# The first group of a projection by seven products, and four fills placed apart

## The chip, the cores and the metric

The kernel runs on one NeuronCore of a Trainium2 chip. Five engines work side by side: TensorE (PE) multiplies matrices, VectorE (DVE) and ScalarE (ACT) work element by element, GpSimd (POOL) and SyncE (SP) mostly start transfers (DMAs). Each engine runs its own instructions strictly in the order in which the program lists them, and semaphores make it wait for others. The metric is the device time of one execution in microseconds (us); lower is better.

## The reference, cut to what matters

One layer of a streaming encoder: six column blocks of one large product of the input x (1024 x 1024) with w_in (1024 x 6144), two mixers on four of them, gates from the other two, an output product and a layer norm.

```python
h = jnp.einsum('bsd,de->bse', x, w_in[l]) + b_in[l]
xa, za, xb, zb, ga, gb = jnp.split(h, splits, axis=-1)
xa = _causal_depthwise_conv(xa, conv_w[l], conv_b[l])
ya = _rg_lru(xa, ...) * jax.nn.silu(za)
yb = _multiscale_pool(xb, w_pool[l], b_pool[l], pool_scale[l]) * jax.nn.silu(zb)
merged = (jax.nn.sigmoid(ga) * jnp.einsum('bsw,wd->bsd', ya, w_proj_a[l])
          + jax.nn.sigmoid(gb) * jnp.einsum('bsw,wd->bsd', yb, w_proj_b[l]))
y = jnp.einsum('bsd,de->bse', merged, w_out[l]) + b_out[l]
x = _layer_norm(DEEPNORM_ALPHA * x + y, ln_gain[l], ln_bias[l])
```

All of it is float32. The kernel keeps that precision by splitting every operand into a high and a low part (high x high, high x low, low x high), so that one product of a 128 x 128 weight block with 512 columns of the input is three matmuls.

## The kernel before

**Groups and seven products.** The large product is cut into 24 groups, listed in `order` (line 601): G0, A0, G1, A1, G2 and so on, then the B groups. A group takes two column blocks of 128 of w_in (`blocks_of`, line 606), each 1024 rows long. With the two halves of the rows as k and the two halves of the 1024 input columns as h, a group is a 2 x 2 by 2 x 2 block product, and it is computed in Strassen's way (Winograd's form) with seven products instead of eight. Each of the seven is four quarters of 128 rows by three passes: 12 matmuls. `Group` (line 530) has them as m1 to m7; m1 and m2 use parts of the weights and the input as they are (blocks 11, and 12 with 21), the others use sums. `Weights` (line 475) makes the weight sums: `step("12")` splits the first raw block `ra`, `step("75")` makes two sums with the second block `rb` and splits them, `step("63")` two more, `step("4")` splits a part of `rb`. A split (line 456) is a cast on ACT for the high part and a subtraction on DVE for the low part. The sums of the input are made once, in the opening, and are used by all groups. What PSUM holds is added up in `a_outputs`, `g_outputs` and `b_outputs` (functions c11, c12, c21, c22), on DVE for the most part; `copied` (line 540) copies PSUM to SBUF on ACT.

**The opening (lines 956 to 1136).** Eight matmuls on zeros (`WARM`) run while the first input lands. G0 is not computed with seven products but plainly: four blocks of weight (`w0r`, split into `w0h`, `w0l`) and four parts of the input in quarters as they arrive, 2 x 2 x 8 x 3 = 96 matmuls into four PSUM banks `ps_s` (`mm0`, `parts`), whose outputs ACT reads directly (`plain`, line 833). Meanwhile DVE and ACT split the input (`x13`, `x2`, `xb`) and make its sums (`t13` for products 5 and 7, `t24` for 6 and 4). Then A0 follows: products 1, 2, 5, 7 and 3 in the opening, 6 and 4 between the products of G1 (`first_rest`).

**The loop (line 1157).** For every further group: weights of the next group, products 1, 2, 7, then the work put off from earlier groups (`between`: gate matmuls `ps_g` of an A group, product 3 of the group before, its end), then products 6, 4, 5. `run_jobs` hands two or three jobs per group to POOL: sums of weight and input blocks in DRAM by adding DMAs. Among the jobs is the input plus the output bias, which the last stage needs: a fill of a DRAM tile `xb` of 1 MB with the bias row (on the SP queue), then an adding DMA of x (on POOL), four times; two of the pairs are queued behind the first weight sums, two behind the group of A3 (`biased_input`, lines 702 and 796).

**What sets the order.** `Plan` (line 162) records all operations, gives each a due time and lays them out in a simulated time. TensorE and POOL keep the order of the program. On ACT, DVE and SP the operation that is due first among those that are ready goes next; `within` (line 180) and `LEAD` set how long an operation may be put off. Its costs are formulas in `cost` (line 220), with a rate of 270 GB/s for the SP queue. The result is one fixed list per engine; on the chip an engine never changes it. Buffers are few: 28 tiles of 4 KB per partition in the pool x, 10 in w, 4 in r, 10 in k (1024 columns of work), 4 of half the size in e, and 8 PSUM banks. A tile that is written waits until the earlier user of its buffer is done, and a store to DRAM counts as a use.

Of the kernel before, what the change touches and what calls it, by code (L numbers as in the profile page):

```python
# [26 lines left out]
WARM = 8  # L27
# [134 lines left out]
class Plan:  # L162
# [10 lines left out]
    @contextmanager  # L173
    def in_order(self, *engines):
        self.chained.append(set(engines))
        yield
        self.chained.pop()
# [229 lines left out]
def layer_kernel(ctx: ExitStack, tc: tile.TileContext, xq, x, w_in, par, wg, w_pool, wpa, wpb, w_out, rows, out):  # L407
# [67 lines left out]
    class Weights:  # L475


        def __init__(self, name, w1, w2):
            self.name, self.out, self.tiles = name, {}, {}
            self.ra, self.rb = rt(f"ra_{name}"), rt(f"rb_{name}")  # L480
            nc.sync.dma_start(self.ra, w1)
            nc.sync.dma_start(self.rb, w2)
# [219 lines left out]
    def biased_input(blocks):  # L702
        for sl in HALF if not src.get("bias") else ():
            src["bias"] = True
# [3 lines left out]
            nc.sync.dma_start(bias_d[:, sl], t)  # L708
        for i in blocks:
# [53 lines left out]
    def a_gates(c, xc, xh, xl, sz):  # L763
# [29 lines left out]
        if c == KQ - 1:  # L793
            input_sums1("a")
            output_sums()
            biased_input((0, 1))
        elif c == NK - 1:
            input_sums2("a")

# [3 lines left out]
    def g_outputs(sec, d):  # L803
# [5 lines left out]
        def c11(ps, m1):  # L809
            V.tensor_tensor(t[0][:, HALF[0]], ps, m1, ALU.add)  # L810

        def c12(ps, rest=None):
            if rest is not None:
                V.tensor_tensor(rest, ps, rest, ALU.add)
                ps = rest
# [11 lines left out]
        def finish():  # L827
            done(0, 0, t[0][:, HALF[0]], 1.0)
            store(0)
# [3 lines left out]
        def plain(i, ps):  # L833
            for h in range(2):
                done(i, h, ps[h], 1.0)
            store(i)
# [4 lines left out]
        finish.plain = plain  # L841
# [114 lines left out]
    begin = ctx.enter_context(ExitStack())  # L956
    pass
# [3 lines left out]
    for i in range(WARM):  # L961
        nc.tensor.matmul(psw, warm[:, 0:P], warm, start=True, stop=True)
    first = blocks_of(*order[0])
    wr, wh, wl = [[f(f"{t}{n}") for n in range(2)] for t, f in
                  (("w0r", lambda n: wt(n, F32)), ("w0h", wt), ("w0l", wt))]
# [4 lines left out]
    xb = [xt(f"xb_{q}") for q in range(KQ)]  # L970

    def w0_part(t, n, a, b):
        return t[n].rearrange("p h (k m) -> p h k m", m=P)[:, :, a:b, :]

    def dma_w0(n, a, b):

        (A if a == 0 else nc.sync).dma_start(w0_part(wr, n, a, b), w_in[first[n]].rearrange("p (h k) m -> p h k m", h=2)[:, :, a:b, :])

    def split_w0(n, a, b):
        split(*(w0_part(t, n, a, b) for t in (wr, wh, wl)))  # L980

    def dma_x(q, i, sl=slice(0, S)):
        nc.sync.dma_start(xr[q][i][:, sl], xq[q, i][:, sl])


    def quarter(q, kh, h):
        if kh == h:
            return x13[q][0][:, kh, :], x13[q][1][:, kh, :]
        t = x2[q] if kh else xb[q]
        return t[:, 0, :], t[:, 1, :]  # L990

    raws = {(0, 0): (0, 0), (1, 1): (0, 1), (0, 1): (1, 0), (1, 0): (1, 1)}

    def split_x(q, kh, h):
        i, p = raws[kh, h]
        split(xr[q][i][:, HALF[p]], *quarter(q, kh, h))

    ps0 = [[bank(f"ps_s{n}_{h}") for h in range(2)] for n in range(2)]

    def mm0(q, kh, h, n):  # L1000
        sl = slice(q * P, (q + 1) * P)
        passes(ps0[n][h], (wh[n][:, kh, sl], wl[n][:, kh, sl]), quarter(q, kh, h),
               q == 0 and kh == h, q == KQ - 1 and kh != h)

    dma_w0(0, 0, 1)
    dma_x(0, 0, HALF[0])
    dma_w0(1, 0, 1)
    dma_x(0, 0, HALF[1])
    dma_x(0, 1, HALF[0])
    dma_x(0, 1, HALF[1])  # L1010
    dma_w0(0, 1, KQ)
    dma_x(1, 0)
    dma_w0(1, 1, KQ)
    dma_x(1, 1)
    for q in range(2, KQ):
        dma_x(q, 0)
        dma_x(q, 1)
    nc.sync.dma_start(par_sb, par)
    softplus()

    X = {j: [None] * KQ for j in range(1, 8)}
    t13, t24 = [None] * KQ, [None] * KQ
    for q in range(KQ):
        X[1][q], X[2][q], X[3][q] = quarter(q, 0, 0), quarter(q, 1, 0), quarter(q, 1, 1)

    x57 = [[xt(f"x57{t}{q}") for t in "hl"] for q in range(KQ)]
    x64 = [[xt(f"x64{t}{q}") for t in "hl"] for q in range(KQ)]
    for q in range(KQ):
        for i, (a, b) in enumerate(((5, 6), (7, 4))):
# [3 lines left out]
    def hi(raw, t):  # L1033
        A.copy(t, raw)

    def lo(raw, t, u):
        V.tensor_tensor(u, raw, t.bitcast(F32), ALU.subtract)

    def sum57(q):
        t13[q] = xt(f"t13_{q}", F32)  # L1040
        r = xr[q][0].rearrange("p (i s) -> p i s", i=2)
        V.tensor_tensor(t13[q], r, xr[q][1][:, HALF[0]].unsqueeze(1).to_broadcast((P, 2, H)), ALU.subtract)

    def hi57(q):
        hi(t13[q], x57[q][0])

    def lo57(q):
        lo(t13[q], *x57[q])

    def sum6(q):  # L1050
        t24[q] = wt(f"t24_{q}", F32)
        V.scalar_tensor_tensor(t24[q][:, 0, :], t13[q][:, 0, :], -1.0, xr[q][0][:, HALF[1]], ALU.mult, ALU.subtract)

    def sum4(q):
        V.scalar_tensor_tensor(t24[q][:, 1, :], t24[q][:, 0, :], -1.0, xr[q][1][:, HALF[1]], ALU.mult, ALU.subtract)

    def hi64(q, i):
        hi(t24[q][:, i, :], x64[q][0][:, i, :])

    def lo64(q, i):  # L1060
        lo(t24[q][:, i, :], *(t[:, i, :] for t in x64[q]))

    def parts(q, between=None):
        r = xr[q][0].rearrange("p (i s) -> p i s", i=2)
        todo = [(r, *x13[q])] + [(xr[q][raws[p][0]][:, HALF[raws[p][1]]], *quarter(q, *p)) for p in ((0, 1), (1, 0))]
        if between is not None:
            split(*todo.pop(0))
            between()
        for raw, t, u in todo:
            hi(raw, t)  # L1070
        for raw, t, u in todo:
            lo(raw, t, u)
        for kh, h in ((0, 0), (1, 1), (0, 1), (1, 0)):
            for n in range(2):
                mm0(q, kh, h, n)

    def each(f, qs, *a):
        for q in qs:
            f(q, *a)

    split_w0(0, 0, 1)
    for kh, h in ((0, 0), (1, 1), (0, 1), (1, 0)):
        split_x(0, kh, h)
        mm0(0, kh, h, 0)
        if kh == h == 1:
# [488 lines left out]
```

## Time and profile before

| what | us |
|---|---|
| median of three runs | 743.36 (742.93 to 745.26) |
| profiled execution | 744.67 |
| its span, first to last instruction | 742.9 |
| PE, DVE, ACT busy | 732.6, 600.5, 458.7 |

The span is from the first to the last instruction on the chip; the execution has about 1.8 us around it. In the views quoted below, columns are start and duration, then the engine and the operation with its output and inputs by the program's names without buffer numbers (so `ra_A` is the first raw block of any A group); a bracket gives the idle time of that engine just before and what ended it. All operations come from one helper, line 394, so tiles tell them apart, not lines. A letter h or l at the end of a name is the high or low part. `SPq` is the queue of SP, where DMAs are started.

### The profile page before, as it was taken

To read this page: it belongs to the slowest core of one execution; us is meant where nothing else is said; L and a number is where in the kernel's file an instruction comes from. 1 tells how busy PE (TensorE), PEld (TensorE's weight loads), DVE (VectorE), ACT (ScalarE), POOL (GpSimd) and SP (SyncE) were. 2 spreads that over 40 slices of the span, in tenths; PEclk is the share of its full clock that TensorE was granted. 3 is DMA by queue.
4 is the path that set the end of the run, shared out by engine and by line. 5 is a ranking of instruction groups with operands and counts; after the bars stand their busy time and mean duration, and the time that the engine had idled before them with its cause. 6 is when DMAs were issued, how large, how long until landed. Compare 5 with 4: busy or idle time off the path is not lost.

```text
span 742.9 us, 8776 instructions
## 1 busy us (share of the span) xinstructions
PE 732.6 (99%) x3248; PEld 599.4 (81%) x3248; DVE 600.5 (81%) x744; ACT 458.7 (62%) x583; POOL 70.0 (9%) x119
## 2 busy tenths in 40 slices
PE   9999999999999999999999999999999999999995
PEld 6888887888888878788788888888888888888885
DVE  7999796969696978884997778879948886999766
ACT  7686959686877868687655445456543545324473
POOL 0171011111100110100110000100000000000031
PEclk9999999999999999999999999999999999999999
DMA  9246868676847998889787714998679997757566
GB/s 341 88 139 180 222 166 231 149 239 163 237 107 208 246 288 271 222 223 261 150 204 136 194 56 157 283 328 317 227 247 302 317 312 245 267 201 254 153 111 116
DMA packets 63523, 158.98 MB, mean 214 GB/s; under 512 B 4276, under 2 KB 7476, under 8 KB 63416
## 3 DMA queue, kind: packets, MB, share of 16 engines
q1 hardware_dynamic: 42824, 106.26, 41.1%
q0 software_dynamic: 20112, 51.91, 33.3%
q8 instruction: 25, 0.41, 0.2%
q10 hardware_dynamic: 544, 0.26, 0.1%
q14 instruction: 18, 0.15, 0.1%
HBM read 137.43 MB, written 77.07 MB: 289 GB/s over the span
## 4 chain that ended last, share of the span: by engine, by line
PE 96%; DVE 1%; DMA 1%; issue 1%; ACT 0%; SPq 0%; DVEq 0%
PE a_A L394 11%; PE a_G L394 10%; PE a_B L394 10%; PE oa L394 6%; PE pa_a L394 6%; PE pa_b L394 6%; PE c_A L394 6%; PE c_B L394 5%; PE c_G L394 5%; PE ps_pool L394 3%; PE oc L394 3%; PE pc_b L394 3%; PE pc_a L394 3%; PE e_B L394 3%; PE e_A L394 3%; PE e_G L394 3%
## 5 line engine op out<-in xcount | busy, mean ns | idle before, releaser
L394 ACT ACT_TABLE_LOAD x38 | 48.8, 1283 | 5.8 <-DMA sg<-sg 3.1
L394 DVE TENSOR_TENSOR i<-i,xc 128x1024 f32<-128x1024 f32 x8 | 9.8, 1225 | 27.1 <-ACT i L394 27.1
L394 DVE SCALAR_TENSOR_TENSOR xc<-xp,par_sb,xc 128x1024 f32<-128x1024 f32 x24 | 30.7, 1281 | 0.3
L394 ACT ACTIVATE zb<-zb,par_sb 128x1024 f32<-128x1024 f32 (+1 forms) x16 | 15.0, 939 | 16.1 <-DVE zb L394 15.9
L394 PE MATMUL pa_a<-oh,oh 128*128 128x512 f32 x64 | 24.9, 389 | 0.0
L394 PE MATMUL pa_a<-oh,ol 128*128 128x512 f32 x64 | 24.9, 389 | 0.0
L394 PE MATMUL pa_b<-oh,oh 128*128 128x512 f32 x64 | 24.9, 389 | 0.0
L394 PE MATMUL pa_b<-ol,oh 128*128 128x512 f32 x64 | 24.9, 389 | 0.0
L394 PE MATMUL pa_b<-oh,ol 128*128 128x512 f32 x64 | 24.9, 389 | 0.0
L394 PE MATMUL pa_a<-ol,oh 128*128 128x512 f32 x64 | 24.9, 389 | 0.0
L394 ACT ACTIVATE r<-ps_g,par_sb 64x512 f32<-64x512 f32 x32 | 21.9, 684 | 2.1 <-PE ps_g L394 1.2
L394 ACT ACTIVATE i<-ps_g,par_sb 64x512 f32<-64x512 f32 x32 | 21.9, 684 | 1.9 <-DVE r L394 1.4
L394 POOL COPY paced<-pace 128x1 f32<-128x1 f32 x18 | 9.7, 541 | 124.4 <-ACT pace L394 124.4
L394 PE MATMUL c_A<-x64h,wd_A 128*128 128x512 f32 x64 | 21.0, 389 | 0.0
L394 PE MATMUL c_B<-x64h,wd_B 128*128 128x512 f32 x64 | 21.0, 389 | 0.0
L394 POOL DMA_DIRECT2D out<-y x7 | 8.5, 1210 | 131.2 <-ACT sd L394 115.7
L394 PE MATMUL ps_pool<-mixh,wp 128*128 128x512 f32 x64 | 20.7, 394 | 0.0
L394 PE MATMUL e_A<-x,wah_A 128*128 128x512 f32 x64 | 19.7, 389 | 0.0
L394 PE MATMUL e_B<-x,wah_B 128*128 128x512 f32 x64 | 19.7, 389 | 0.0
L394 PE MATMUL c_G<-x64h,wd_G 128*128 128x512 f32 x56 | 18.4, 389 | 0.0
L394 DVE TENSOR_TENSOR_SCAN r<-a,i 128x1024 f32<-128x1024 f32 x8 | 18.3, 2284 | 0.1
L394 PE MATMUL e_G<-x,wah_G 128*128 128x512 f32 x56 | 17.2, 389 | 0.0
(521 smaller groups left out, 2536.7 us busy)
## 6 DMA issues: line engine op xcount, KB each, us to landing
sg<-sg SPq DMA_DIRECT2D x16, 512.0 KB, 4.0
ra_A<-in_w_in SPq DMA_DIRECT2D x8, 512.0 KB, 3.4
rb_A<-in_w_in SPq DMA_DIRECT2D x8, 512.0 KB, 8.6
ya<-r SPq DMA_DIRECT2D x8, 512.0 KB, 8.6
xb<-bias SPq DMA_DIRECT2D x4, 1024.0 KB, 13.4
xb<-in_x POOLq DMA_DIRECT2D x4, 1024.0 KB, 9.9
ra_B<-in_w_in SPq DMA_DIRECT2D x8, 512.0 KB, 7.5
rb_B<-in_w_in SPq DMA_DIRECT2D x8, 512.0 KB, 6.7
```

Source lines behind the costliest of these rows:

```text
L394: getattr(getattr(nc, t.op[0]), t.op[1])(*a, **k)
```

## The change

G0 is now computed with seven products like the other groups. The opening runs product 1 of G0 and A0 by quarters as the first quarter-blocks of the input land, product 1 of G1 and A1, product 2 of the four in the same order, then products 5, 7, 3, 6 and 4 of G0 and A0, one after the other for both. The sums of the input are made in between, in pieces of 512 columns, and partly in place of the raw input. The first raw block of each of the four groups is loaded and split early (`early`); for G1 and A1 it is loaded a second time later, for the sums. The order of the input loads follows. The zero matmuls are six instead of eight. G groups of the opening store the first half tile separately (`ahead`), since the work tiles are taken by the raw input until the sums are done. In the loop, groups 2 and 3 go on at product 7. The bias row is made after the opening, and each of the four fills stands at a place of its own, at groups 3, 4, 9 and 10, with a leeway of 25 us; two of the additions of x come after all sums of the A branch.

```diff
-WARM = 8
+WARM = 6
...
-    def load_group(i, w=None, todo=("12", "4", "75", "63")):
-        w = w or weights_steps(i)
-        for js in ("4", "75", "63 apart", "12") if i >= len(order) - 2 else todo:
+    def load_group(i):
+        w = weights_steps(i)
+        for js in ("4", "75", "63 apart", "12") if i >= len(order) - 2 else ("12", "4", "75", "63")[i < 4:]:
             w.step(js)
...
+    def fill_bias(i):
+        with nc.within(LEAD):
+            nc.sync.dma_start(xb_d[i], bias_d.to_broadcast((2 * P, D)))
...
     def biased_input(blocks):
         for i in blocks:
-            def both(i=i):
-                nc.sync.dma_start(xb_d[i], bias_d.to_broadcast((2 * P, D)))
-                add_to(xb_d[i], x[2 * P * i:2 * P * (i + 1), :])
-            jobs.append(both)
+            jobs.append(lambda i=i: add_to(xb_d[i], x[2 * P * i:2 * P * (i + 1), :]))
...
         def c11(ps, m1):
-            V.tensor_tensor(t[0][:, HALF[0]], ps, m1, ALU.add)
+            if ahead:
+                V.tensor_tensor(m1, ps, m1, ALU.add)
+                A.activation(m1, m1, AF.Sigmoid, bias=pcol(C_BIN + sec, d))
+                nc.sync.dma_start(sg_d[sec][d][:, HALF[0]], m1)
+            else:
+                V.tensor_tensor(t[0][:, HALF[0]], ps, m1, ALU.add)
...
+    load_w(0, 0, 0, 1, A)
+    dma_x(0, 0, HALF[0])
+    load_w(1, 0, 0, 1, A)
+    for i in range(2):
+        load_w(i, 0, 1, KQ)
+        dma_x(i + 1, 0, HALF[0])
+    dma_x(3, 0, HALF[0])
...
+    for q in range(KQ):
+        split(B11[q], *X[1][q])
+        for i, g in enumerate(groups[:2]):
+            if q < 2:
+                split_w(i, 0, *((0, 1), (1, KQ))[q])
+            part(g, g.a, 1, q, True, False)
+    for i, g in enumerate(groups[:2]):
+        g.t1 = g.copied("m1", g.a)
+    for i in (2, 3):
+        split_w(i, 0, 0, KQ)
+        groups[i].m1()
+
+    t13 = [xt(f"t13_{q}", F32) for q in range(KQ)]
+    with nc.within(SOON):
+        for q in range(KQ):
+            V.tensor_tensor(t13[q][:, 0, :], B11[q], B12[q], ALU.subtract)
+            split(t13[q][:, 0, :], *X[5][q])
+    es = [bank(f"e_{g.name}") for g in groups[:2]]
+    for q in range(KQ):
+        split(B21[q], *X[2][q])
+        for i, g in enumerate(groups[:2]):
+            if q == 0:
+                split_w(i, 1, 0, KQ)
+            part(g, es[i], 2, q, True, True)
+    for g, e in zip(groups, es):
+        g.take(0, e, g.t1)
+    for i in (2, 3):
+        split_w(i, 1, 0, KQ)
+        groups[i].m2()
+    w = [Weights("%s%d" % order[i], early[i][1], w_in[blocks_of(*order[i])[1]]) for i in range(2)]
+    f5, t5 = [], []
+    for i, g in enumerate(groups[:2]):
+        w[i].step("4")
+        w[i].step("75")
+        g.w.update(w[i].out)
+        f5.append(bank(f"f_{g.name}"))
+        g.mul(f5[i], 5, True, False)
+        t5.append(g.copied("m5", f5[i]))
+    for q in range(KQ):
+        V.tensor_tensor(t13[q][:, 1, :], B22[q], B12[q], ALU.subtract)
+        split(t13[q][:, 1, :], *X[7][q])
+    for i, g in enumerate(groups[:2]):
+        g.m7()
+    for q in range(KQ):
+        split(B22[q], *X[3][q])
+    for i, g in enumerate(groups[:2]):
+        w[i].step("63")
+        g.w.update(w[i].out)
+        V.tensor_tensor(t5[i], t5[i], g.t7, ALU.add)
+        g.mul(f5[i], 3, False, True)
+    for q in range(KQ):
+        V.scalar_tensor_tensor(B22[q], t13[q][:, 0, :], -1.0, B22[q], ALU.mult, ALU.subtract)
+        split(B22[q], *X[6][q])
+    for i, g in enumerate(groups[:2]):
+        g.m6()
+        g.take(1, f5[i], g.u2)
+        g.take(3, g.a, t5[i])
+    for q in range(KQ):
+        V.scalar_tensor_tensor(B21[q], B22[q], -1.0, B21[q], ALU.mult, ALU.subtract)
+        split(B21[q], *X[4][q])
+    for g in groups[:2]:
+        g.m4()
...
+    FILLS = {3: 2, 4: 3, 9: 0, 10: 1}
     for i in range(1, len(order)):
         kind, c = order[i]
+        if i in FILLS:
+            fill_bias(FILLS[i])
...
-            g.m1()
-            g.m2()
+            if i >= 4:
+                g.m1()
+                g.m2()
```

More of the change, by code (lines that the diff above doesn't have):

```diff
@@ L175, in in_order @@
         self.chained.append(set(engines))
+        for e in engines:
+            self.last.pop(e, None)
         yield
@@ L969, in layer_kernel @@
     x2 = [xt(f"x2_{q}") for q in range(KQ)]
[L970 to L1024, printed above, removed]
     x57 = [[xt(f"x57{t}{q}") for t in "hl"] for q in range(KQ)]
     x64 = [[xt(f"x64{t}{q}") for t in "hl"] for q in range(KQ)]
+    X = {j: [None] * KQ for j in range(1, 8)}
     for q in range(KQ):
+        X[1][q] = x13[q][0][:, 0, :], x13[q][1][:, 0, :]
+        X[3][q] = x13[q][0][:, 1, :], x13[q][1][:, 1, :]
+        X[2][q] = x2[q][:, 0, :], x2[q][:, 1, :]
         for i, (a, b) in enumerate(((5, 6), (7, 4))):
@@ L1050, in sum6 @@
[L1050 to L1075, printed above, removed]
@@ new lines, in layer_kernel @@
+    for i in range(2):
+        load_w(i, 1, 0, KQ)
+    for q in range(KQ):
+        dma_x(q, 1, HALF[1])
+    load_w(2, 0, 0, KQ)
+    load_w(2, 1, 0, KQ)
+    for q in range(KQ):
+        dma_x(q, 1, HALF[0])
+        dma_x(q, 0, HALF[1])
+    load_w(3, 0, 0, KQ)
+    load_w(3, 1, 0, KQ)
+    softplus()
+    tiles, groups, outs = {}, [], {}
+    for i in range(4):
+        kind, c = order[i]
+        if kind == "A":
+            tiles[i], takes = a_outputs(c)
+        else:
+            outs[i], takes = g_outputs(GA, c, True)
+        groups.append(Group("%s%d" % order[i], early[i][3], X, *takes))
@@ new lines, in part @@
+    def part(g, ps, j, q, first, last):
+        sl = slice(q * P, (q + 1) * P)
+        passes(ps, tuple(t[:, sl] for t in g.w[j]), X[j][q], first and q == 0, last and q == KQ - 1)
+    for g in groups[:2]:
+        g.a = bank(f"a_{g.name}")
+    for q in range(KQ):
[6 more added lines that the diff above has]
+        g.t1 = g.copied("m1", g.a)
```

183 lines of the change are left out of this document (60 added, 123 removed).

## The prediction

> **What bounds the kernel now.** I read the busy shares of the page first, then what TensorE waited for.
>
> ```profile
> PE 732.6 (99%) x3248; PEld 599.4 (81%) x3248; DVE 600.5 (81%) x744; ACT 458.7 (62%) x583; POOL 70.0 (9%) x119
> ```
>
> ```profile
> PE ps_warm L394 <- DVE xp L394: 1.4, 1, 1.4
> PE a_B L394 <- DVE zb L394: 0.8, 1, 0.8
> PE a_B L394 <- ACT u_B L394: 0.4, 1, 0.4
> ```
>
> TensorE (PE) is busy 99% of the span and waits three times in all, so only three things can gain: fewer matmuls, an earlier first one, the two waits at a_B. But the average hides the opening. The table by stretch (columns: busy time and instructions of PE, weight load, VectorE = DVE, ScalarE = ACT, POOL; clock; DMA share; GB/s) shows it:
>
> ```profile
> 1.00:3.00 2.00, 1.55 (x4) 1.26 (x5) 0.40 (x2) 0.95 (x1) 0.25 (x9) 1.00 0.49 154
> 3.00:5.00 2.00, 2.00 (x6) 1.54 (x5) 0.93 (x2) 1.68 (x4) 0.00 (x0) 1.00 1.02 325
> 5.00:10.00 5.00, 5.00 (x20) 3.95 (x18) 3.33 (x6) 3.02 (x6) 0.00 (x0) 1.00 1.04 377
> 10.00:20.00 10.00, 9.85 (x42) 7.28 (x41) 10.00 (x12) 8.47 (x12) 0.00 (x0) 1.00 1.03 407
> 20.00:30.00 10.00, 10.00 (x46) 8.29 (x45) 9.97 (x13) 6.52 (x8) 0.00 (x0) 1.00 0.13 51
> 30.00:40.00 10.00, 10.00 (x46) 8.29 (x45) 9.95 (x16) 7.52 (x10) 5.19 (x9) 1.00 0.16 54
> 40.00:50.00 10.00, 10.00 (x46) 8.28 (x45) 8.79 (x13) 9.09 (x17) 8.67 (x17) 1.00 0.29 113
> 50.00:60.00 10.00, 10.00 (x46) 8.29 (x45) 9.97 (x15) 5.20 (x8) 2.00 (x4) 1.00 0.77 255
> 70.00:80.00 10.00, 10.00 (x50) 7.75 (x49) 5.94 (x8) 9.70 (x15) 1.20 (x2) 1.00 0.62 191
> ```
>
> From 10 to 60 us DVE is as full as PE; it has air only from 70 us on. DMA is full until 20 us and then nearly idle; ACT is never the fullest. So what is added to DVE in the opening is as dear as a matmul. This is where the change works.
>
> **The units.** Timelines of PE, DVE and ACT (start, us, engine, what), and the chain:
>
> ```profile
> 1.45 3.78 PE L394 MATMUL ps_warm<-warm 128*128 128x512 f32 x8 [1.45 <-DVE xp L394]
> 5.03 0.63 PE L394 MATMUL ps_s<-x13h,w0h 128*128 128x512 f32 x1
> 6.73 0.40 PE L394 MATMUL ps_s<-x13l,w0h 128*128 128x512 f32 x1
> 6.96 0.39 PE L394 MATMUL ps_s<-x13h,w0l 128*128 128x512 f32 x1
> ```
>
> ```profile
> 3.94 0.40 ACT L394 CAST w0h<-w0r 128x256 fp32r<-128x256 f32 x1
> 4.07 0.69 DVE L394 TENSOR_TENSOR x13l<-xr,x13h 128x512 fp32r<-128x512 f32 x1 [2.67 <-ACT x13h L394]
> 11.37 1.82 DVE L394 TENSOR_TENSOR w0l<-w0r,w0h 128x768 fp32r<-128x768 f32 x2
> 29.47 1.22 DVE L394 TENSOR_TENSOR wbl_A<-sb_A,wbh_A 128x1024 fp32r<-128x1024 f32 x1
> 30.60 1.22 DVE L394 TENSOR_TENSOR x57l<-t,x57h 128x1024 fp32r<-128x1024 f32 x1
> 34.24 0.75 DVE L394 SCALAR_TENSOR_TENSOR xp<-e_A,par_sb,m_A 128x512 f32<-128x512 f32 x1
> 34.91 0.68 DVE L394 SCALAR_TENSOR_TENSOR t<-t,xr 128x512 f32<-128x512 f32 x1
> 42.17 2.51 DVE L394 TENSOR_TENSOR x64l<-t,x64h 128x512 fp32r<-128x512 f32 x4 [0.84 <-ACT x64h L394]
> 46.24 0.69 DVE L394 TENSOR_TENSOR rb_G<-ra_G,rb_G 128x512 f32<-128x512 f32 x1
> 46.96 0.69 DVE L394 TENSOR_TENSOR ra_G<-rb_G,ra_G 128x512 f32<-128x512 f32 x1
> ```
>
> ```profile
> 28.77 2.72 PE a_A L394 x12
> 72.28 1.59 PE ps_g L394 x12
> ```
>
> A product of 12 matmuls takes 2.72 us (0.227 each). The first real ones come every 0.42 us, (6.73 - 5.03) / 4, about 0.2 lost on each. On DVE an operation of 512 columns takes 0.605 us of the engine ((2.51 - 0.69) / 3), of 1024 columns 1.13 (29.47 to 30.60), a sum in place on the one before it 0.72 (46.24 to 46.96), an addition from PSUM with bias 0.67 (34.24 to 34.91).
>
> **The change part by part.** (1) G0 as seven products: 84 matmuls instead of 96, minus 12 x 0.227 = -2.7 us. (2) Two warm-up matmuls fewer: the eight start 0.43 apart, so six end near 4.0. The first weight piece is 128 columns instead of 256; already the larger was cast at 4.34 and its matmul only waited for the warm-up. I take 4.6 as first matmul against 5.03: -0.4. (3) What the opening now does: products 1 of G0 and A0 by quarters as the input lands, products 1 of G1 and A1, products 2 in the same order (96 matmuls), then 5, 7, 3, 6, 4 of G0 and A0 (120).
>
> Arrival: the first 24 matmuls need 1.57 MB, 1.31 of it up to A0's second weight piece. The rows moved 0.31 + 0.65 = 0.96 MB by 5.0 and then 377 GB/s, so that piece is over at 5.9; with about 1 us to land (the third row of the queue is full all this time), cast and subtraction of 384 columns (0.45 each, half of the 768-column row) its high half is there near 8.0, and PE, having come to it at 7.6 or earlier, loses some 0.7 us. All else then lands earlier than it is used: 96 matmuls take 22 us, the 407 GB/s row brings 4 MB in 10. So products 2 of G0 and A0 are over at T4 = 4.6 + 72 x 0.227 + 5 x 0.2 + 0.7 = 22.6. Its ends: a start at 4.3 with no loss gives 21.6; a start at 5.03 and twice the loss 23.7.
>
> Up to T4 DVE has 4 quarters x 4 subtractions or differences (16 x 0.605, products 1, 2 and 5), the low halves of the weights (3.8 with G1's first half and one second half): about 14 us from 4.07 on, with some 2 us lost to arrivals, over at 20. It then meets the additions from PSUM of product 2, which need T4; the weight sums stand behind them, because the planner puts their raw block, last but one in the SP queue, later than T4 (its queue rate is 270, the trace's 407; I take only the order from that). DVE stands idle for 2 to 3 us, and everything after T4 is a chain through it:
>
> - additions of product 2, four groups: 2 x 0.605 + 2 x 0.67 = 2.6; one low half of A1's weights 0.6
> - weights 4, 7, 5 of two groups: 2 x (0.605 + 2 x 0.72 + 1.13) = 6.4
> - inputs 7: 4 differences, 4 low halves = 4.8; inputs 3: 2.4
> - weights 6, 3: 2 x (2 x 0.72 + 1.13) = 5.1; the two sums t5: 1.2
> - inputs 6: 8 x 0.605 = 4.8; four outputs of products 3 and 5: 2.5; inputs 4: 4.8
>
> The sum is 35.2 us. From T4 to the matmul that takes the last low half of input 4, PE has ten products (2 of G1 and A1, then 5, 7, 3, 6 of G0 and A0) and ten matmuls of G0's product 4: 10 x 2.72 + 10 x 0.227 = 29.5. So PE waits 5.7 us in the course of products 3, 6 and 4, and ends product 4 of A0 at 22.6 + 35.2 + 0.45 + 2.72 = 61.0. Five more products (G1's 7, 6, 4, 5, A1's 7) bring the gate matmuls ps_g to 74.6; in the trace they stand at 72.28, with the same products before them. The opening gives +2.3: of DVE work it carries G0's seven weights and its outputs, which the old form had on ACT or not at all. Before, the same sum leaves PE unstopped because 96 plain matmuls ran ahead of the first sums.
>
> (4) Moves that I cost at nothing: G1's and A1's first block is read twice (1.05 MB, 2.6 us of queue at 407 GB/s, from about 40 us on, where the DMA share is 0.29; without that cover their weights 4 to 6 us late). G0 and G1 store half a tile early, with two more table loads on ACT (the page's row below has 1.28 each, under ACT's free third). Biases of the input leave the opening. POOL's additions change order only after the weight sums.
>
> (5) The fills. These are SP, DVE, PE and POOL rows around the two waits at a_B, and two rows of the page:
>
> ```profile
> 323.07 1.22 SPq L394 DMA_DIRECT2D xb<-bias  x2
> 339.72 1.45 SPq L394 DMA_DIRECT2D sg<-sg  x2
> 352.76 0.69 DVE L394 TENSOR_TENSOR zb<-c_B,u_B 128x512 f32<-128x512 f32 x1 [5.17 <-DMA sg<-sg]
> 354.10 0.50 PE L394 MATMUL a_B<-x13h,wch_B 128*128 128x512 f32 x1 [0.75 <-DVE zb L394]
> 354.26 1.04 POOL L394 DMA_DIRECT2D xb<-in_x  x1 [14.32 <-issue]
> 362.93 0.50 PE L394 MATMUL a_B<-x57h,wbh_B 128*128 128x512 f32 x1 [0.37 <-ACT u_B L394]
> ```
>
> ```profile
> L394 ACT ACT_TABLE_LOAD x38 | 48.8, 1283 | 5.8 <-DMA sg<-sg 3.1
> ...
> xb<-bias SPq DMA_DIRECT2D x4, 1024.0 KB, 13.4
> ```
>
> Two fills of 1 MB go out at 323; the store of G7 behind them, at 339.72, lands only at 352.76 and holds a work tile that DVE needs. PE loses 0.75 and, still catching up, 0.37. The change takes the fills away from there (groups 3, 4, 9, 10), and the addition of the input at 354 with its twin behind it. Bounds: 0 gained if POOL's adding DMAs of that stretch alone held the store, 1.1 if the fills did; I take -1.1.
>
> **Sum.** Opening +2.3 (in it the 12 matmuls, the earlier start and the waits), fills -1.1: +1.2. The span goes from 742.9 to 744.1; the profiled execution is 744.67, 1.8 around its span, so 745.9. It is 1.3 above the median of the runs; on 743.36 I predict **744.6**. About 2.2 us (0.3%) is what a measurement tells from no change, so this is no change.
>
> **Rivals.**
> A, all of DVE's work hides: then ps_g follows PE alone, 22.6 + 12 x 2.72 + 13.6 = 68.8, -3.5, with the fills -4.6: 738.8. For it: DVE was full before too and stopped nothing. Against: 35.2 is more than 29.5 by the same rows.
> B, the weight sums come ahead of the additions and fill the 2.5 us before T4: ps_g at 72.1, -0.2, with the fills -1.3: 742.1.
> C, the slower side: the fills of groups 3 and 4 hit the stretch after the opening, where DVE is late. A store or load within 13.4 us behind a fill lands late, as the store of 339.72 did by 13 us; it costs from the point where DVE wants its tile sooner than that. Price 1.1 each as at a_B, two of them: 746.8. The DMA share of 0.62 there speaks against, the full DVE for it.
> D, the clock: the slow spacing lasted 5.3 us of unbroken matmuls (1.45 to 6.73). If the gap from 4.0 to 4.6 makes it start anew, it lasts until 9.9, 3.2 us more at 0.42 instead of 0.227: 1.5 us on T4 and all behind it: 746.1. The profile's clock column says 1.00 in these rows, so the spacing alone shows it. [...]
> E, the fills were not the cause at a_B, the edit does not do what it says there: +1.1, 745.7.
>
> **How the numbers follow.** Forecast 0.42 (743.2 to 746.0), A 0.10, B 0.20, C 0.15, D 0.06, E 0.07. Below 741.1: A, and 0.06 of B for a shorter wait still. Above 745.6: 0.10 of the forecast (1 us more idle on DVE), most of C, D and E: 0.32. The rest 0.52. Range 740.4 to 747.4: it leaves out A and the upper part of C, some 0.18 in all, and within it lie both ends of T4 (1 us each way) and the ends of the chain: 2.5 us less idle as in B, some 2 us more if DVE also waits for ACT's casts.
>
> **What would show it.** PE waiting for DVE some 5 us in products 3, 6 and 4 of G0 and A0; DVE idle just before the additions of product 2; ps_g's first matmul near 74.6; no wait of PE at a_B near 350. If PE's waits in the opening sum to under 2 us, the chain through DVE was wrong; if ps_g is right and the end is not, the fills were.

## The result and the profile after

The changed kernel takes **752.3 us** (median; four runs from 750.39 to 753.63) against 743.34 before: the ratio is 1.0113, interval 1.0096 to 1.0131. I had predicted 744.6, in a range of 740.4 to 747.4. It is slower, and outside the range. The profiled execution took 751.0, its span 749.2 (before 744.67 and 742.9), so the profile shows 6.3 us of the loss. The four runs lie at two levels, about 750.7 and 753.6; what the upper one is comes with the experiments.

What TensorE waited for in the changed kernel (line 396 is the helper that was line 394):

```profile
PE c_G L396 <- DVE x64l L396: 2.9, 2, 1.5
...
PE e_G L396 <- ACT x L396: 1.2, 1, 1.2
PE f_G L396 <- DVE x13l L396: 1.0, 1, 1.0
PE a_G L396 <- ACT x13h L396: 0.6, 1, 0.6
PE f_A L396 <- DVE wbl_A L396: 0.5, 1, 0.5
PE c_G L396 <- DVE wbl_G L396: 0.5, 1, 0.5
PE e_G L396 <- DVE x L396: 0.2, 1, 0.2
```

The two waits at a_B are gone. In their place stand 6.9 us of waits (the table is of the waits by tile, with the total, the number and the longest; the row left out is that of the warm-up, the same as before), nearly all in the opening: in front of product 1 (a_G) and in products 2 (e_G), 5 (f_A), 3 (f_G) and 4 (c_G). The first gate matmul after the opening and two later markers show where the time went in; the timeline of PE gives the first, the chain of waits the others:

```profile
79.45 0.50 PE L396 MATMUL ps_g<-xch,gh 64*128 64x512 f32 x2
```

```profile
407.69 5.56 PE ps_pool L396 x24
664.38 22.15 PE oa L396 x96
```

ps_g stood at 72.28 before: the opening alone costs 7.2 us, where I had 2.3. The same markers of the kernel before were 401.30 and 657.54: the difference is 6.4 at ps_pool and 6.8 at oa. So after the opening little is lost, and some of the loss is got back at a_B. The table by stretch (columns as before):

```profile
5.00:10.00 5.00, 5.00 (x11) 3.69 (x12) 3.41 (x7) 3.14 (x7) 0.00 (x0) 1.00 0.96 300
10.00:15.00 5.00, 5.00 (x23) 4.13 (x22) 2.39 (x5) 3.15 (x6) 0.00 (x0) 1.00 1.05 393
15.00:20.00 5.00, 3.81 (x17) 2.81 (x15) 3.96 (x8) 2.99 (x6) 0.00 (x0) 1.00 1.04 395
20.00:30.00 10.00, 9.78 (x41) 7.54 (x41) 9.96 (x18) 7.17 (x12) 0.08 (x1) 1.00 0.34 123
...
50.00:60.00 10.00, 8.56 (x36) 5.97 (x34) 9.78 (x17) 5.13 (x9) 6.06 (x13) 1.00 0.00 0
```

DVE is busy 9.76 of the 15 us from 5 to 20 and then without a break, while PE thins out from 15 on. Three places in the timelines of PE, ACT and DVE say why.

```profile
4.96 0.80 PE L396 MATMUL a_G<-x13h,wah_G 128*128 128x512 f32 x1 [0.59 <-ACT x13h L396]
...
9.69 0.50 PE L396 MATMUL a_A<-x13l,wah_A 128*128 128x512 f32 x1
10.02 0.39 PE L396 MATMUL a_A<-x13h,wal_A 128*128 128x512 f32 x1
...
12.77 0.39 PE L396 MATMUL a_A<-x13h,wal_A 128*128 128x512 f32 x1
19.79 0.50 PE L396 MATMUL e_G<-x,wah_G 128*128 128x512 f32 x1 [1.20 <-ACT x L396]
25.92 0.39 PE L396 MATMUL e_A<-x,wal_A 128*128 128x512 f32 x1
62.43 0.49 PE L396 MATMUL c_G<-x64l,wd_G 128*128 128x512 f32 x1 [1.49 <-DVE x64l L396]
```

```profile
12.51 0.59 ACT L396 COPY m_G<-a_G 128x512 f32<-128x512 f32 x1 [1.51 <-PE a_G L396]
18.63 0.59 ACT L396 COPY m_A<-a_A 128x512 f32<-128x512 f32 x1 [1.09 <-PE a_A L396]
19.12 1.14 ACT L396 CAST x<-xr 128x512 fp32r<-128x512 f32 x2
```

```profile
9.02 0.69 DVE L396 TENSOR_TENSOR x13l<-xr,x13h 128x512 fp32r<-128x512 f32 x1 [1.59 <-ACT x13h L396]
14.34 0.69 DVE L396 TENSOR_TENSOR wal_G<-ra_G,wah_G 128x512 fp32r<-128x512 f32 x1 [2.61 <-ACT wah_G L396]
19.77 1.29 DVE L396 TENSOR_TENSOR x<-xr,x 128x512 fp32r<-128x512 f32 x2 [0.82 <-ACT x L396]
61.70 0.68 DVE L396 TENSOR_TENSOR x64l<-xr,x64h 128x512 fp32r<-128x512 f32 x1
```

First, PE's spacing stays at 0.43 until 10.0 (before: until 6.73), and the 24 first matmuls end at 13.0 instead of the 11.7 that my terms give. Second, ACT works its list in order: copies of finished products stand ahead of casts whose input is there (e6 below shows that it is), so ACT idles 1.51 and 1.09 us for PE; the cast of input 2 comes at 19.12, PE waits for it, and DVE has idled 2.61 us for the cast of G1's weights. Third, the last low half of input 4 is made at 61.70, and PE, waiting 1.44 and 1.49 us in G0's product 4, takes it at 62.43. From there to ps_g it is 17.0 us of products.

### The profile page after: what moved, and what is told of

Read it like the earlier page. It is cut to its first block, busy times and chain, and to the rows that moved or that the text cites. A ratio compares the mean times of both kernels' runs of the same rounds, so it can differ in the third digit from the quotient of the medians.

```text
span 749.2 us, 8807 instructions
## 1 busy us (share of the span) xinstructions
PE 733.5 (98%) x3234; PEld 596.5 (80%) x3234; DVE 605.4 (81%) x766; ACT 462.9 (62%) x596; POOL 71.6 (10%) x118
## 4 chain that ended last, share of the span: by engine, by line
PE 88%; DVE 7%; ACT 3%; issue 1%; DMA 0%; DVEq 0%; ACTq 0%
PE a_B L396 11%; PE a_A L396 10%; PE a_G L396 10%; PE oa L396 6%; PE pa_a L396 6%; PE pa_b L396 6%; PE c_B L396 6%; PE c_A L396 4%; PE c_G L396 4%; PE ps_pool L396 3%; PE oc L396 3%; PE pc_b L396 3%; PE pc_a L396 3%; PE e_B L396 3%; PE e_A L396 2%; PE e_G L396 2%
## 5 line engine op out<-in xcount | busy, mean ns | idle before, releaser
L396 PE MATMUL e_G<-x,wah_G 128*128 128x512 f32 x64 | 20.4, 394 | 1.4 <-ACT x L396 1.2
L396 PE MATMUL c_G<-x64h,wd_G 128*128 128x512 f32 x64 | 21.0, 389 | 0.0
L396 POOL COPY paced<-pace 128x1 f32<-128x1 f32 x17 | 8.2, 484 | 116.9 <-ACT pace L396 116.9
```

The costliest lines, as they stand in the source:

```text
L396: getattr(getattr(nc, t.op[0]), t.op[1])(*a, **k)
```

## The experiments

Times are medians; the ratio is to the kernel before on the same chip (its medians were 743.34 beside the changed kernel and 744.0 to 744.8 beside the others). ps_g is its first start in the profiled execution. e9 to e12 come after the others.

| run | us | ratio, interval | ps_g |
|---|---|---|---|
| changed kernel | 752.3 | 1.0113 (1.0096 to 1.0131) | 79.45 |
| e1_fills_only | 742.79 | 0.9983 (0.9974 to 0.9991) | 71.96 |
| e2_opening_only | 751.56 | 1.0109 (1.0087 to 1.0131) | 82.4 |
| e3_warm8 | 751.41 | 1.0102 (1.0082 to 1.0121) | 82.8 |
| e4_copies_late | 751.3 | 1.010 (1.008 to 1.012) | 79.5 |
| e5_less_dve | 744.65 | 1.0003 (0.9994 to 1.0013) | 74.42 |
| e6_plan_rate | 751.67 | 1.0112 (1.0088 to 1.0135) | 78.95 |
| e7_kept_busy | 751.34 | 1.0098 (1.0083 to 1.0113) | 81.1 |
| e8_both | 741.71 | 0.9971 (0.9959 to 0.9984) | 71.23 |
| e9_pool_rate | 748.49 | 1.0056 (1.0034 to 1.0078) | 78.0 |
| e10_pool_only | 755.79 | 1.0148 (1.0125 to 1.017) | 82.2 |
| e11_no_gap | 749.71 | 1.0076 (1.0054 to 1.0098) | 78.23 |
| e12_no_gap_rate | 749.98 | 1.0102 (1.0056 to 1.0148) | 76.41 |

### The two halves apart

e1 is the kernel before with the fills of the changed one; e2 is the changed kernel with the fills of the one before. With the fills go the additions of x on POOL: out of the jobs of A3's group, behind the weight sums. The parts of e1's edit that matter:

```diff
-            def both(i=i):
-                nc.sync.dma_start(xb_d[i], bias_d.to_broadcast((2 * P, D)))
-                add_to(xb_d[i], x[2 * P * i:2 * P * (i + 1), :])
-            jobs.append(both)
+            jobs.append(lambda i=i: add_to(xb_d[i], x[2 * P * i:2 * P * (i + 1), :]))
...
-            biased_input((0, 1))
         elif c == NK - 1:
             input_sums2("a")
+            biased_input((0, 1))
...
+    FILLS = {3: 2, 4: 3, 9: 0, 10: 1}
     for i in range(1, len(order)):
...
+        if i in FILLS:
+            fill_bias(FILLS[i])
```

> The kernel before with nothing changed but the fills and additions of the biased input, placed as in the change. If the two fills at 323 us held the store of G7 and so the two waits at a_B, both waits go and the time falls by about 1.1 us, to 742.2, with the gate matmuls of A0 still at 72.3 us. If the waits came from POOL's adding DMAs, they stay and the time is 743.3. If the fills at groups 3 and 4 hurt what follows the opening (rival C), the time rises by 1 to 2 us.

> The changed kernel with the fills as they were before. If the opening alone makes the loss, the gate matmuls of A0 stand at about 79.4 us as in the changed kernel and the time is 1.1 to 1.7 us above it, 753.4 to 754. If the early fills make the loss, the time falls back to 744 to 746.

e1 gains 1.2 us (742.79 against 744.02), e2 loses 7.5. In the old opening the moved fills bring the predicted time, and the loss is the opening's: e2 has it without them. The waits of e1, all of them:

```profile
PE ps_warm L394 <- DVE xp L394: 1.4, 1, 1.4
PE ps_s L394 <- DVE xb L394: 0.3, 1, 0.3
PE ps_s L394 <- DVE x13l L394: 0.2, 1, 0.2
PE ps_s L394 <- ACT x13h L394: 0.2, 1, 0.2
```

Nothing waits at a_B. But e1 does not tell the fills from POOL's adding DMAs, since both moved: the 1 MB sum p4o<-p2o, which before goes out at 338.72, one us ahead of the store of G7, goes out at 310.08 in e1. And e2, with the old fills, has no wait of PE at a_B either, and misses its expected 753.4 to 754:

```profile
359.47 0.69 DVE L396 TENSOR_TENSOR zb<-c_B,u_B 128x512 f32<-128x512 f32 x1 [2.20 <-DMA sg<-sg]
```

There the two fills go out at 318.86, the sum at 347.31 and the store at 350.67. By then the fills have landed (17.5 us at the longest in this run), and DVE still waits 2.20 us for the store, which PE does not feel. So which of the two DMAs held the store in the kernel before stays open, and so does what the moved fills are worth on top of the new opening.

The profiled execution of e2 took 754.71, one of the upper level, and its table by stretch shows what that is (clock third from the end):

```profile
55.00:60.00 5.00, 3.81 (x16) 2.51 (x14) 5.00 (x9) 2.76 (x6) 1.96 (x6) 1.00 0.00 0
60.00:65.00 5.00, 3.27 (x8) 2.31 (x9) 4.96 (x8) 3.73 (x5) 0.00 (x0) 0.66 0.02 4
65.00:70.00 5.00, 5.00 (x16) 3.96 (x15) 3.06 (x5) 2.60 (x3) 0.00 (x0) 0.65 0.61 175
```

The granted clock falls to 0.66 and 0.65, and from the second wait on the matmuls of e2 stand 0.43 apart again:

```profile
60.24 0.50 PE L396 MATMUL c_G<-x64l,wd_G 128*128 128x512 f32 x1 [1.43 <-DVE x64l L396]
62.70 0.80 PE L396 MATMUL c_G<-x64l,wd_G 128*128 128x512 f32 x1 [1.50 <-DVE x64l L396]
63.72 0.63 PE L396 MATMUL c_A<-x64h,wd_A 128*128 128x512 f32 x1
64.15 0.63 PE L396 MATMUL c_A<-x64l,wd_A 128*128 128x512 f32 x1
```

This goes on to 68.4: 13 matmuls lose 0.2 each, 2.6 us, most of the 2.9 between the two levels of the changed kernel. There too the granted clock goes with the level: over the whole execution it is 0.993 and 0.992 in the two upper runs, 0.999 and 0.998 in the two lower ones. So it looks like a second price of the same two waits. No single gap of PE there was longer than 1.50 us, so for this kernel two waits close together went with the fall, in some executions.

### The number of warm-up matmuls, and the copies

e3 takes back the eight warm-up matmuls; e4 asks for the two copies of product 1 only after product 2.

```diff
-WARM = 6
+WARM = 8
```

```diff
-    for i, g in enumerate(groups[:2]):
-        g.t1 = g.copied("m1", g.a)
...
     for g, e in zip(groups, es):
+        g.t1 = g.copied("m1", g.a)
         g.take(0, e, g.t1)
```

> The changed kernel with eight matmuls on zeros instead of six. If the gap before the first product keeps TensorE at its slow spacing until 10 us, the spacing turns near 6.7 us as before the change, the first 24 matmuls end some 1.3 us earlier and the time falls by 1.3 us, to 751.0. If VectorE's list decides, which stands idle for other reasons up to 20 us, the spacing turns earlier but the gate matmuls of A0 stay near 79.4 us and the time stays at 752.3.

> The changed kernel with the copies of product 1 out of PSUM asked for later (behind product 2 in the program), so that ScalarE's casts of weights and input no longer stand behind copies that wait for TensorE. If these copies starve VectorE (2.6 us idle from 11.7 to 14.3 us, 0.8 near 19) and TensorE (1.4 us at 18.4), the gate matmuls of A0 come 2.5 to 3 us earlier, near 76.7 us, and the time falls to 749.5. If VectorE's sum of work behind product 2 alone decides, nothing changes.

Neither moves the time (751.41 and 751.3 against 752.3). In e3 the first real matmul is at 5.03 but the second waits 0.55 for DVE to 6.29, and the spacing stays slow until 10.7: the loss is not the number. e4 tested nothing: in its trace the copies stand where they stood (ACT's at 12.53 and 18.65), because the planner orders ACT by the arrivals it expects and not by the program's order. e6 therefore changes those arrivals.

### VectorE's list, ScalarE's order, and both

e5 lets ACT write the low halves of inputs 7, 3, 6 and 4 by a cast (16 DVE operations less); the subtraction is left out, so these halves don't hold the low parts, and e5 and e8 are no versions to use. e6 tells the planner that SP's queue moves 400 GB/s instead of 270. e8 does both.

```diff
-        split(t13[q][:, 1, :], *X[7][q])
+        for t in X[7][q]:
+            A.copy(t, t13[q][:, 1, :])
...
-        split(B21[q], *X[4][q])
+        for t in X[4][q]:
+            A.copy(t, B21[q])
```

```diff
-BANDWIDTH = {"SP": 270e3, "ACT": 270e3, "POOL": 120e3}
+BANDWIDTH = {"SP": 400e3, "ACT": 270e3, "POOL": 120e3}
```

> The changed kernel with the low halves of inputs 7, 3, 6 and 4 written by a cast on ScalarE in place of a subtraction on VectorE (so those halves hold the wrong values): 16 x 0.605 = 9.7 us less in VectorE's list behind product 2, 16 x 0.52 = 8.3 us more on ScalarE. If VectorE's sum of work is what stops TensorE, the waits at f_G and c_G (3.9 us) go, the gate matmuls of A0 come near 75.5 us, and the slow clock after those waits goes too: 746.5 with a spread under 1 us. If the waits come from something else (buffers, arrivals, ScalarE), they stay and the time is 751 to 754.

> The changed kernel with 400 in place of 270 GB/s as the planner's rate of the SP queue; only the fixed order of each engine changes. If ScalarE's casts stood behind the copies of product 1 because the plan had the input land later than it does, the wait at e_G (1.4 us) goes, VectorE idles some 3 us less before 20 us, and its list ends 3 us earlier: gate matmuls of A0 near 76.5 us, time 749 or less. If the order makes no difference, 751 to 754.

> The lighter VectorE list of e5_less_dve and the planner's rate of e6_plan_rate together (low halves of inputs 7, 3, 6, 4 hold the wrong values). If VectorE's list and the order of casts are all that the opening loses, nearly all waits go: gate matmuls of A0 near 71 to 72 us, the 12 matmuls saved show at last, and the time is 740 to 742, under that of the kernel before. If something else holds the opening (slow spacing up to 10 us, arrivals), it stays above 743.

e5 comes out at the time of the kernel before (744.65, there 744.36); its ten runs lie within 1.9 us, without the upper level. e6 alone gains nothing, though ACT's casts of G1's weights and of input 2 start at 11.51 and 16.61 instead of 13.68 and 19.12, and product 2's end is at 23.99 instead of 26.15. e8 is 2.6 us faster than the kernel before (744.36 to 741.71). The rows of the waits that tell, of e5, of e6 and of e8 (all but the warm-up's):

```profile
PE e_G L396 <- ACT x L396: 1.2, 1, 1.2
...
PE c_G L396 <- ACT x64h L396: 0.3, 1, 0.3
```

```profile
PE c_G L396 <- DVE x64l L396: 2.9, 2, 1.5
PE oa L396 <- DVE z L396: 1.5, 1, 1.5
```

```profile
PE a_G L396 <- ACT wah_G L396: 0.8, 1, 0.8
PE f_A L396 <- DVE wbl_A L396: 0.5, 1, 0.5
```

With DVE lighter the waits of products 3 and 4 vanish, with the planner's rate the one of product 2; only with both does the opening gain. At ps_g it gains 1.0 us (71.23 against 72.22), not the 2.7 of 12 matmuls; the rest of the 2.6 comes later, where e1 had its 1.2. In e6 the waits at c_G are the same 2.9, three us earlier. It also has a new wait of 1.5 at oa, since the rate reorders the rest of the kernel too, and in its profiled execution the clock fell after the waits.

### TensorE kept busy through the waits

e7 puts six small matmuls of zeros, 32 stationary columns each, in front of quarters 3 and 4 of G0's product 4.

```diff
-        g.m4()
+        for q in range(KQ):
+            if g is groups[0] and q >= 2:
+                for _ in range(6):
+                    nc.tensor.matmul(g.c[0:32, :], zero, X[1][0][0], start=False, stop=False, skip_group_check=True)
+            part(g, g.c, 4, q, False, True)
+        g.take(2, g.c, g.u2)
```

> The changed kernel with 6 matmuls on zeros (they add nothing) ahead of the third and the fourth quarter of G0's product 4, where TensorE otherwise waits 1.44 and 1.49 us for VectorE. If the runs near 753.6 are those in which these waits let the clock fall (spacing 0.43 from 62.7 us on, granted clock 0.65), no run is above 751.5 and the spread is under 1.5 us, at 750 to 751. If the two levels have another cause, about half of the runs stay near 753.5.

No run is at the upper level: four runs from 751.17 to 751.71, where the changed kernel has 750.39 to 753.63. DVE's list is as before, so the time is that of the lower level and the added matmuls. That supports that the level is the clock after the waits; four runs, where two of four or two of six were at the upper level without the matmuls, don't prove it.

### Eight operations on GpSimd

e9 (with e6's rate) and e10 (with the old one) are a try at a usable version: the second halves of the input sums and the weight sums for products 6 and 3 go from VectorE to GpSimd.

```diff
-        V.tensor_tensor(t13[q][:, 1, :], B22[q], B12[q], ALU.subtract)
+        nc.gpsimd.tensor_tensor(t13[q][:, 1, :], B22[q], B12[q], ALU.subtract)
...
-        w[i].step("63")
+        w[i].sums63(None, nc.gpsimd)
+        w[i].split("wc", w[i].sa, (6, 3))
...
-    softplus()
-
...
+    softplus()
     load_g(0)
```

> Correct values. The changed kernel with the plan's transfer rate of e6_plan_rate (the casts of input 2 ahead of the copies) and with eight subtractions and additions of 128x512 (the second halves of the four sums for products 7 and 3, and the four sums of weights for products 6 and 3 of G0 and A0) given from VectorE to GpSimd, which does little before 70 us; the softplus terms follow them on GpSimd. At 0.605 us of spacing VectorE has 8 x 0.605 = 4.8 us less in front of the last low half of input 4. Theory (VectorE's list behind the end of products 2 holds TensorE, and the casts' order adds to it): with both lightened as in e8_both, but by less (there 16 instructions, here 8), the waits at f_G and c_G fall from about 6 us to 0 to 2 us, the first ps_g comes at 72 to 75, and the time at 742 to 745, if GpSimd's 128x512 operation takes under about 1.5 us. Rival (GpSimd is too slow, or slows VectorE while both read memory): a GpSimd operation over 2 us or VectorE's spacing above 0.61 beside it; products 7 and 6 wait for GpSimd, ps_g at 78 or later, the time 749 or more.

> Correct values. e9_pool_rate with the plan's old transfer rate: the copies stand before the casts as in the changed kernel, eight operations of 128x512 are on GpSimd. Theory: the waits at e_G (about 1.2) and the later end of products 2 stay, the list behind it is 4.8 us shorter: waits at f_G and c_G 0 to 2 us, ps_g at 74 to 77, the time 744 to 747, so e5_less_dve's effect in part with right values. Rival (GpSimd too slow or in VectorE's way): 749 or more, as in e9_pool_rate.

The theory's numbers failed: 748.49 and 755.79, against 742 to 745 and 744 to 747. GpSimd is not too slow by itself (1.3 to 2.2 us an operation, mostly 1.6), but DVE is held up beside it. From e10's timelines:

```profile
21.77 6.41 POOL L396 TENSOR_TENSOR t<-xr,xr 128x512 f32<-128x512 f32 x4 [20.53 <-DMA xr<-in_xq]
21.87 1.80 DVE L396 TENSOR_TENSOR x<-xr,x 128x512 fp32r<-128x512 f32 x1
...
25.28 1.75 DVE L396 TENSOR_TENSOR x<-xr,x 128x512 fp32r<-128x512 f32 x1
26.95 1.78 DVE L396 TENSOR_TENSOR wd_G<-rb_G,wd_G 128x512 fp32r<-128x512 f32 x1
28.77 0.69 DVE L396 TENSOR_TENSOR rb_G<-rb_G 128x512 f32<-128x512 f32 x1
```

Four GpSimd operations fill 6.4 us, 1.6 each, and each of the four DVE operations beside them lasts 1.75 to 1.80 instead of 0.69: in the time of one GpSimd operation DVE loses 1.1 us, nearly twice the 0.605 that moving it saves. From 20 to 30 us DVE is as full as in the changed kernel, but with 11 instructions instead of 18. To the end of the last low half of input 4 (from 4.4 us on) DVE is busy 52.6 us in e9 and 54.1 in e10, where the changed kernel has 52.0: the eight operations fewer saved nothing. The four have both inputs in SBUF; additions with one input in PSUM lasted no longer beside GpSimd operations than in the changed kernel (in e9 0.68 us for m_G<-e_G at 26.62 and 0.74 for xp<-e_A at 28.42). Why the others are held up no run shows. In e9, in addition, PE waited 3.55 us in product 5 for low weights, and its clock in the 15 us from 30 on was 0.77. It is still 3.2 us faster than e6; it has neither e6's waits at c_G nor the one at oa.

### No gap in front, and whose end counts

e11 fills the gaps in front of the first products: eight warm-up matmuls, and three more between the first and second real one. e12 has e6's rate as well.

```diff
+            if q == 0 and i == 0:
+                (wh, wl), (mh, ml) = [t[:, 0:P] for t in g.w[1]], X[1][0]
+                nc.tensor.matmul(g.a, wh, mh, start=True, stop=False, skip_group_check=True)
+                for _ in range(3):
+                    nc.tensor.matmul(psw, warm[:, 0:P], warm, start=True, stop=True)
+                nc.tensor.matmul(g.a, wh, ml, start=False, stop=False, skip_group_check=True)
+                nc.tensor.matmul(g.a, wl, mh, start=False, stop=False, skip_group_check=True)
+                continue
             part(g, g.a, 1, q, True, False)
```

> The changed kernel with eight warm-up matmuls again, and three more between the first and the second matmul of G0's product 1, so that TensorE has no idle time in front of the products. In the kernel before TensorE worked without a gap from 1.45 and its spacing fell from 0.43 to 0.23 at 6.73, after 5.3 us; in the changed kernel it was idle for 0.59 at 4.37 to 4.96 and again for some 0.3 at 5.4 to 5.68, and the spacing fell at 10.0, 4.3 us after the second; with eight warm-ups it was idle 0.55 to 6.29 and the spacing fell at 10.7, 4.4 us after that. Theory (a short gap starts the slow stretch anew): without gaps the spacing falls by 6.8 to 7.2, the 24 first matmuls end about 12.0 (13.0 in the changed kernel), and products 2 end earlier only if ACT's casts let them; the time 750 to 752, since the casts at 19 and VectorE's list stay. Rival (real products, not gaps, keep the spacing slow): it falls at 10 or later.

> e11_no_gap with the plan's transfer rate of e6_plan_rate, so that the casts of input 2 stand ahead of the copies: both halves of the later end of products 2 (26.15 against my 22.6) are taken away, VectorE's list is left as it is. Theory (VectorE's list behind the end of products 2 makes the loss, the late end only adds to it): products 2 end near 23 to 24, the waits at f_G and c_G stay at 4 us or more or grow, since TensorE comes to them earlier, and the time stays at 749 to 752. Rival (the late end of products 2 was the cause): the waits shrink with it and the time falls to 746 or below.

In e11 the spacing is short from 5.3 to 6.0 on, and product 2 ends 1.2 us earlier; so does everything up to ps_g (78.23 for 79.45), and the time is 749.71. In e12 product 2 ends at 24.44, 1.7 earlier than in the changed kernel, and the waits at c_G are still 2.9; the one at f_G is gone, so the 4 us or more that were expected there did not stay. ps_g is 1.8 earlier than in e11 and the time is the same, since e12 has, like e6, a new wait at oa, of 1.6. What is constant is DVE. DVE's busy time from 4.4 us to the end of the last low half of input 4, in the changed kernel, in e6, in e11 and in e12 (columns: stretch, its length, DVE busy and count, clock, DMA share, GB/s):

```profile
4.40:62.38 57.98, 52.05 (x86) 1.00 0.45 161
```

```profile
4.40:59.24 54.84, 51.95 (x86) 0.99 0.49 171
```

```profile
4.40:61.17 56.77, 51.97 (x86) 1.00 0.46 165
```

```profile
4.40:59.34 54.94, 51.93 (x86) 1.00 0.48 170
```

Four programs, each 86 operations and 52.0 us of work; only the idle time differs: 5.9, 2.9, 4.8 and 3.0. Since the work is the same, the end of the list, 4.4 + 52.0 + idle, moves with DVE's idle time (by -3.0, -1.1 and -2.9 against the changed kernel, the ends by -3.1, -1.2 and -3.0); it goes less well with the end of product 2 (-2.2, -1.2, -1.7).

## Why the prediction was wrong

**The mechanism was right in the main.** I said that PE would wait for DVE in products 3, 6 and 4 behind a chain that PE's products don't cover. It does: 0.95 in product 3 and 2.93 in product 4 in the trace, none in product 6, together 3.9 where I had 5.7; and e5 and e8, which lighten just that chain, remove these waits and the loss. The sign of the opening was right too: later, not earlier, in spite of 12 matmuls less.

**Which step failed.** Step (3), the opening, by its size: ps_g at 79.45 where I had 74.6. By the prediction's own terms: T4, the end of product 2, is 25.92 + 0.23 = 26.15 instead of 22.6, which is 3.5 us. The list behind it ends at 62.38, 36.2 after T4 against 35.2, another 1.0. From there to ps_g it is 17.1 against 16.8, the last 0.3. So the term most wrong is T4, the opening ahead of the chain; the chain itself was off by 1.0.

T4 came late for two reasons. The 24 first matmuls ended 1.3 us late: I had given five of them the slow spacing, eleven had it, and the first started at 4.96 instead of 4.6. The 0.7 that I had put on A0's second weight piece, with 1 us of landing that I took without a row, did not come: its cast ran at 6.09, not near 8.0. (For the landing, the trace of before has this: the last load of its opening, rb_G, goes out at 13.34 and lands 9.1 us later, at 22.4, while the DMA share falls from 1.04 just before 21.0 to 0.05 between 21.6 and 22.0.) And after product 1 of A1 the next matmul started at 19.79 instead of some 18.4, since ACT's cast of input 2 stood behind a copy that waited for PE; the quarters of product 2 lost the rest, 0.9. I had ACT in the sum only as a time per operation and as "ACT is never the fullest": an engine that is a third idle still holds others up, if what stands at the head of its list waits.

**But T4 was also the wrong hinge.** I let DVE stand idle until T4 and then counted 35.2 us from there. The trace has DVE idle earlier, in three pieces of 1.59, 2.61 and 0.82 us from 7.4 to 19.8, each ended by an ACT cast (the first of these casts itself waited for its input to land, until 8.37). From 19.8 on it has no idle time worth a row, so the idle time just before the additions of product 2, one of my own signs, is not there: the first weight sums run ahead of these additions as in rival B. It did not help, since the work has to be done anyway. The count that holds in all four programs above is that of DVE: I had 14 + 35.2 = 49.2 us of work and 4.5 of idle time from 4.07 on; it is 52.0 and 5.9 from 4.40 on. The 2.9 that I missed in the work are above all operations that the planner puts in between: a low half and two sums of G1's weights at 57.43, 58.63 and 59.84 (1.8). The low halves of the weights took 5.3 where I had 3.8 and 0.6, and small terms 0.4; against these stands that I had rounded up to the 14. My units were right (0.605 for 512 columns).

From this also follows, as a reckoning that was not tried alone: with no idle time at all the list would end at 56.4 and ps_g would start 17.1 later, at 73.5, still behind the 72.0 to 72.3 of the old opening. With this list the changed opening can't gain. It takes less work on DVE ahead of the last low half: e8 has it, and its ps_g is at 71.23. An order that puts the 1.8 us of G1's weights behind that low half is the other way, and no run tried it.

**The rivals.** D, the clock, came true in the profiled execution to the tenth: slow until 9.9 was forecast, 10.0 is seen. In four profiles without a gap in front of the products (before, e1, e11, e12) the spacing is short from 4.8 to 6.7 on; in eight with a gap of 0.4 to 0.8 us (the changed kernel, e2 to e8) only from 9.7 to 11.0 on. But e9 and e10 have the gap too, and their spacing is short from 5.6 and 6.1 on, as e10's timeline of PE shows here, so a gap makes it likely and doesn't make it so:

```profile
5.08 0.50 PE L396 MATMUL a_G<-x13h,wah_G 128*128 128x512 f32 x1 [0.71 <-ACT x13h L396]
...
6.14 0.39 PE L396 MATMUL a_G<-x13h,wal_G 128*128 128x512 f32 x1
6.37 0.40 PE L396 MATMUL a_A<-x13h,wah_A 128*128 128x512 f32 x1
```

What decides between the two stays open. I gave D 0.06, an estimate that no row of before backs, and treated it as an alternative to the forecast; it was to be added to it. Its price is what e11 gets back at ps_g, 1.2 us, where I had 1.5. And I asked only what the clock does before the first product, not what it does after the waits that I had forecast; that, as far as the runs show, is the upper level, some 3 us in two of the four runs.
C did not happen: e2 without the new fills loses as much as the changed kernel. A is refuted by the waits at c_G.

**The fills, step (5), were right in their time.** -1.1 forecast, -1.2 measured in e1 (743.42 was its slowest of twelve runs), so of E the second half falls: the edit does what it says. That the fills, and not POOL's adding DMAs, held the store is not shown, since e1 moved both.

**The sum.** Against the predicted span of 744.1 the profile has 749.2: 4.8 of the 5.1 are the opening, the rest is small losses behind it, such as a wait of 0.5 at c_G near 98 us. The median is 1.3 above the profiled execution because two of the four runs lie at the upper level, and 1.3 I had taken off for the median of before.

**The version that beats both** is e1, the old opening with the new places of the fills: 742.79, ratio 0.9983 (0.9974 to 0.9991). e8 is faster still, but leaves out part of the computation.

## What to carry to other kernels

Where two engines are full side by side, count the whole list of the second engine, from its first operation to the one that the first engine must have, with all that a planner puts in between, and add its idle time. An event in the middle of the list, such as T4, is no safe starting point. An engine with spare time belongs in that sum as well, by what stands at the head of its list: a copy that waits for a product delays the cast behind it, and so both other engines (here ACT idled 1.51 and 1.09 us at such copies). When a forecast has waits in it, ask what the clock does after them (here 0.66 in one profile and 1.00 in another).

## What the runs showed of the hardware

After two waits of 1.43 and 1.50 us within 5 us the granted clock of TensorE fell to 0.66 in the profiled execution of e2; after waits of 1.44 and 1.49 in that of the changed kernel it stayed at 1.00, though two other runs of the same program have the lower mean clock and the longer time. With small matmuls in the waits none of four runs had the longer time. The clock column says 1.00 from 5 to 10 us in the changed kernel although the matmuls stand 0.43 apart: there only the spacing shows the slow stretch.

Four subtractions of 128x512 on GpSimd took 1.6 us each, and the VectorE operations of 512 columns beside them, with two inputs in SBUF, 1.75 to 1.80 instead of 0.69 (e10); with one input in PSUM one took 0.68 beside them (e9). Work moved from VectorE to GpSimd while VectorE was full cost more there than it saved: eight operations fewer left VectorE busy for 52.6 and 54.1 us where the changed kernel has 52.0.
